# Preparing the delta-rule scan inside the projection loop, with low-rank products of 32 rows

## The chip, the cores and the metric

The kernel runs on one core of a Trainium2 chip. The metric is the device time of one execution in microseconds (us); a run's figure is the median of its executions. TensorE (PE) does the matrix products, VectorE (DVE), ScalarE (ACT) and GpSimd (POOL) the elementwise work, and SyncE (SP) issues the transfers from DRAM. Each engine executes its own queue in order; semaphores hold an instruction back until what it needs is there.

## The reference, cut to what matters

The whole program is two transformer-like blocks for 256 context and 256 latent tokens (512 columns together) of width 1024, in float32. The change touches only the mixer of the first block, which sends one projection through two state scans:

```
z = h @ w_in                                    # 1024 -> 26 tiles of 128 columns
z_rw = centred_shift(z[:, :RW_COLS], mu)         # delta rule ("rwkv") part
r, k, v, lw, la, lg = split(z_rw)
logw  = w0 + tanh(lw_d) @ w_up_d                 # two directions d, 32 -> 512
decay = exp(-exp(-softplus(-logw) - 0.5))
iclr  = sigmoid(a0 + la_d @ a_up_d)              # 32 -> 512
kk    = k * k_k / max(norm per head, 1e-12)
k_dir = k * (1 + (iclr - 1) * k_a)
delta-rule scan over (r, decay_d, k_dir_d, v, -kk, kk * iclr_d), forward and backward
zg, xbc, dt = split(z[:, RW_COLS:])              # state space ("mamba") part
xm, B, C = silu(conv(xbc));  chunked state space scan, forward and backward
out = concat([rwkv part, mamba part]) @ w_out
```

Behind the mixer come a gated feed-forward, a neighbourhood attention, a mixture of eight experts and two blocks of another kind; nothing in them is edited.

## The kernel before, in words

`mixer_in` runs over the 26 column tiles of the projection. For a tile b it splits the weights into a high and a low part (`split`, L347 on ACT and L348 on DVE), multiplies them with the split activations (`mm3`, L361, L362 and L364: 24 matmuls of 128x512), and shifts or convolves the result (L475 to L492). Tiles 0 and 1 hold the small inputs `lg`, 2 to 9 `xbc`, 10 to 13 `zg`, 14 to 17 k, 18 to 21 r, 22 to 25 v of the delta rule (`zrw`, 12 tiles).

Beside the tiles a generator, `mamba`, is advanced: L493 says by how many stages after which tile. It has 23 stages: 3 of set-up, taken at tiles 1, 3 and 5, then 20, of which one or two are taken after each tile from the 9th on:

```
for _ in range(1 if b in (1, 3, 5) else 0 if b < 9 else 1 if b % 3 else 2):
    next(beside, None)
```

Of these, `pre` transposes a token block, `seg` makes a decay matrix (L568 and L570 scale masks into `ta` on ACT and POOL, L571 multiplies them on PE, L573 takes the exponential), `out` multiplies (L580, L582), `carry` moves the state, `gate` (L615 to L618) and `group` (L624 to L630, with a reciprocal on DVE at L628) finish it.

`rwkv_prep` comes after the loop. It needs k and `lg` only, not r and v. It loads the low-rank weights `lora` (L650) and overwrites `lg[:, 0]` by a second load once `tl` has been made of it (L661), sums the squares of k per head with four products (L666, `sel`), takes root and reciprocal (L668 to L670), and for each of four column tiles j and two directions d makes: a low-rank product and sigmoid for the decay (L675, L677), its running sum in chunks of 64 (L679, a scan on DVE into `cs`), a low-rank product and sigmoid `ic` (L682, L683), `kd` = `ic` scaled and shifted (L685) times k (L686), and, once a product of 8 rows has spread the norms (L688) and k is normalised (L689), `b` = k times `ic` (L691, on POOL). The weights of each low-rank product are stored with zeros in the other 96 rows, so that every product reads all 128 rows of `tl`. The ring `pq` of two buffers holds the squares, the norms and the decay's sigmoids in turn; `ic0` and `ic1` have two buffers each.

`rwkv` then scans eight chunks. Its head fills `X` and `bkp` on POOL (L707, L709), and `products` makes `ew`, `ei`, `ar` and `bkp` (L732 to L741) for PE's first products (L750). Beside the scan the rows of the modulation (`ada`, L396 to L405) are computed from transfers of 256 KB each (L329).

Outside of `start`, Tile's scheduler sets each engine's order from a model of its own: it moves instructions across the program's order as their inputs come ready, so the order of the code is only its priority.

Of the kernel before, what the change touches and what calls it, by code (L numbers as in the profile page):

```python
# [11 lines left out]
F32 = mybir.dt.float32  # L12
F32R = mybir.dt.float32r
AF = mybir.ActivationFunctionType
ALU = mybir.AluOpType
# [3 lines left out]
P = 128  # L19
T = 512  # L20
# [73 lines left out]
def host_arrays(inp):  # L94
# [75 lines left out]
    lo = _Pack()  # L170
    for d in range(2):
        lo.add(f"w_up{d}", _rows_to(g["rw_w_up"][0, d], at=32 * d))
        lo.add(f"a_up{d}", _rows_to(g["rw_a_up"][0, d], at=64 + 32 * d))
    lo.add("g_up", _rows_to(g["rw_g_up"][0]))
# [91 lines left out]
class Net:  # L266
# [190 lines left out]
    def mixer_in(self, a, accs, zrw, xbc, zg, lg, pool, beside):  # L457
# [5 lines left out]
        for b in range(26):  # L463
# [20 lines left out]
            else:  # L484
# [6 lines left out]
                for d in range(2):  # L491
                    nc.vector.scalar_tensor_tensor(y, pad[:, :, 2 * d:2 * d + S], self.p(f"mu{d}", j), y,  # L492
                                                   op0=ALU.mult, op1=ALU.add)  # L493
            for _ in range(1 if b in (1, 3, 5) else 0 if b < 9 else 1 if b % 3 else 2):
                next(beside, None)
# [148 lines left out]


    def rwkv_prep(self, zrw, lg, arr, pool):
        nc = self.nc
        mm = nc.tensor.matmul
        lora = pool.tile([P, 2048], F32, name="lora", bufs=1)
        nc.sync.dma_start(lora, self.ins["lora"][:, :2048])  # L650
        o = {n: a for n, (a, _) in self.lora_at.items()}
        reset = pool.tile([P, T], F32, name="reset", bufs=1)
# [7 lines left out]
        nc.vector.tensor_scalar(ka1, self.p("k_a"), -1.0, 1.0, op0=ALU.mult, op1=ALU.add)  # L660
        nc.sync.dma_start(lg[:, 0], self.ins["lora"][:, 2048:2560])  # L661
        ssp = self.bank(2, [8, T])
        for j in range(4):
            kq = pool.tile([P, T], F32, name="pq")
            nc.scalar.activation(kq, zrw[:, j], AF.Square, scale=self.p("k_k", j))
            mm(ssp, self.c("sel")[:, 8 * j:8 * j + 8], kq, start=j == 0, stop=j == 3)  # L666
        nrm = pool.tile([8, T], F32, name="pq")
        nc.scalar.activation(nrm, ssp, AF.Sqrt)  # L668
        nc.vector.tensor_scalar(nrm, nrm, 1e-12, None, op0=ALU.max)
        nc.vector.reciprocal(nrm, nrm)  # L670
        for j in range(4):
            ic = [pool.tile([P, T], F32, name=f"ic{d}") for d in range(2)]
            for d in range(2):
                wp = self.bank(0, [P, T])
                mm(wp, lora[:, o[f"w_up{d}"] + j * P:o[f"w_up{d}"] + (j + 1) * P], tl, start=True, stop=True)  # L675
                sg = pool.tile([P, T], F32, name="pq")
                nc.scalar.activation(sg, wp, AF.Sigmoid, bias=self.p(f"w0{d}", j))  # L677
                back = slice(None, None, -1) if d else slice(None)
                nc.vector.tensor_tensor_scan(arr["cs"][:, d, j, back], reset, sg[:, back], 0.0,  # L679
                                             op0=ALU.mult, op1=ALU.add)  # L680
                ap = self.bank(1, [P, T])
                mm(ap, lora[:, o[f"a_up{d}"] + j * P:o[f"a_up{d}"] + (j + 1) * P], tl, start=True, stop=True)  # L682
                nc.scalar.activation(ic[d], ap, AF.Sigmoid, bias=self.p(f"a0{d}", j))  # L683
                kd = arr["kd"][:, d, j]
                nc.vector.tensor_scalar(kd, ic[d], self.p("k_a", j), ka1[:, j:j + 1], op0=ALU.mult, op1=ALU.add)  # L685
                nc.vector.tensor_mul(kd, kd, zrw[:, j])  # L686
            rp = self.bank(3, [P, T])
            mm(rp, self.c("selt")[0:8, j * P:(j + 1) * P], nrm, start=True, stop=True)  # L688
            nc.vector.scalar_tensor_tensor(zrw[:, j], zrw[:, j], self.p("k_k", j), rp, op0=ALU.mult, op1=ALU.mult)  # L689
            for d in range(2):  # L690
                nc.gpsimd.tensor_mul(arr["b"][:, d, j], zrw[:, j], ic[d])  # L691

    def rwkv(self, zrw, arr, lg, y, pool, fill):
# [256 lines left out]
    def layer0(self, run, late):  # L950
# [3 lines left out]
        with ExitStack() as mix:  # L954
            lgp = pool(mix, "lgp")
            scan = self.consts(mix, "scan")
            lg = lgp.tile([P, 2, T], F32, name="lg")
            zrw = pool(mix, "zp").tile([P, 12, T], F32, name="zrw")
            with ExitStack() as ph:
                self.stream(ph, 4, 1024, side="right")  # L960
                ap = pool(ph, "ap", side="right")
                with ExitStack() as first:
                    a, accs = self.start(zrw, xin, ap, first)
                self.places = cycle([self.raw])
                nc.sync.dma_start(scan, self.ins["cst_scan"])
                mw, mz = pool(ph, "mw", 2), pool(ph, "mz")
                xbc = mz.tile([P, 8, T], F32, name="xbc")
                zg = mz.tile([P, 4, T], F32, name="zg")
                self.mixer_in(a, accs, zrw, xbc, zg, lg, pool(ph, "zw", 2, "right"), self.mamba(xbc, zg, lg, cat, mw, mz))
            with ExitStack() as ph:  # L970
                self.stream(ph, RAWS, 512, 0, "right")
                arrp = pool(ph, "arr", side="right")
                arr = {k: arrp.tile([P, 2, 4, T], F32, name=k) for k in ("cs", "b", "kd")}
                with ExitStack() as c:
                    self.rwkv_prep(zrw, lg, arr, pool(c, "pw", 2))
                with ExitStack() as c:
# [1070 lines left out]
```

## Time and profile before

| what | value |
|---|---|
| median of 3 runs | 3050.53 us (3050.32 to 3051.49) |
| the profiled execution's own time | 3049.11 us |
| its span in the profile | 3047.3 us |
| busy: PE, DVE, ACT, POOL | 96%, 69%, 52%, 25% of the span |
| mean granted TensorE clock | 0.979 |

The profiled execution has its own time beside the span: 1.8 us lie around the span, and it is 1.4 us under the median. The shares are averages over stages with different limits, so they say little of one stage; a stage is read from its own window. A matmul's end is modelled, so that a PE that issues without a gap shows as fully busy.

### The profile page before, as it was taken

To read this page: it belongs to the slowest core of one execution; us is meant where nothing else is said; L and a number is where in the kernel's file an instruction comes from. 1 tells how busy PE (TensorE), PEld (TensorE's weight loads), DVE (VectorE), ACT (ScalarE), POOL (GpSimd) and SP (SyncE) were. 2 spreads that over 40 slices of the span, in tenths; PEclk is the share of its full clock that TensorE was granted. 3 is DMA by queue.
4 is the path that set the end of the run, shared out by engine and by line. 5 is a ranking of instruction groups with operands and counts; after the bars stand their busy time and mean duration, and the time that the engine had idled before them with its cause. 6 is when DMAs were issued, how large, how long until landed. Compare 5 with 4: busy or idle time off the path is not lost. (4 is left out here: it accounts for less than half of the span.)

```text
span 3047.3 us, 44960 instructions
## 1 busy us (share of the span) xinstructions
PE 2935.5 (96%) x17880; PEld 2453.4 (81%) x17880; DVE 2113.2 (69%) x2953; ACT 1592.5 (52%) x2007; POOL 774.2 (25%) x719
## 2 busy tenths in 40 slices
PE   7997899999999998999999999999999999999998
PEld 5884677887888777888888888878888888888887
DVE  5658987622223654998888898977697666669665
ACT  5644223432222555777777776755445545545553
POOL 0335442211022112000000000035264534434552
PEclk9998799999999999999999999999999999999999
DMA  6222234244423334999999999955533555553453
GB/s 229 70 66 70 84 111 148 104 166 146 137 75 114 110 97 154 346 359 331 363 345 337 357 350 362 340 176 186 197 132 120 192 175 199 170 195 107 150 176 128
DMA packets 132456, 584.75 MB, mean 192 GB/s; under 512 B 11792, under 2 KB 48912, under 8 KB 79760
## 3 DMA queue, kind: packets, MB, share of 16 engines
q1 hardware_dynamic: 126592, 575.35, 53.2%
q10 hardware_dynamic: 5648, 6.47, 0.9%
q8 instruction: 142, 2.33, 0.3%
q14 instruction: 74, 0.61, 0.1%
HBM read 580.73 MB, written 1.05 MB: 191 GB/s over the span
## 5 line engine op out<-in xcount | busy, mean ns | idle before, releaser
L348 DVE TENSOR_TENSOR wlo<-raw,whi 128x2048 fp32r<-128x2048 f32 (+2 forms) x497 | 1059.3, 2139 | 243.3 <-ACT whi L347 204.9
L347 ACT ACTIVATE whi<-raw 128x2048 fp32r<-128x2048 f32 (+2 forms) x500 | 886.5, 1784 | 418.8 <-PE bank L362 195.6
L372 PE MATMUL bank<-a,whi 128*128 128x512 f32 x1408 | 355.4, 395 | 5.1 <-DVE a L1693 5.1
L372 PEld LDWEIGHTS bank<-a,whi 128*128 128x128 f32 x1408 | 256.0, 190 | 51.7 <-DVE a L1693 5.4
L1361 PE MATMUL bank<-whi,xghi 128*128 128x512 f32 x704 | 282.3, 401 | 0.0
L1362 PE MATMUL bank<-whi,xglo 128*128 128x512 f32 x704 | 276.6, 393 | 0.0
L348 POOL TENSOR_TENSOR wlo<-raw,whi 128x2048 fp32r<-128x2048 f32 x3 | 13.9, 4646 | 790.2 <-ACT whi L347 790.2
L361 PE MATMUL bank<-cathi,whi 128*128 128x512 f32 (+1 forms) x608 | 212.6, 368 | 1.4 <-ACT x L1264 1.0
L362 PE MATMUL bank<-catlo,whi 128*128 128x512 f32 (+1 forms) x608 | 211.6, 364 | 1.5 <-DVE catlo L454 1.5
L375 PEld LDWEIGHTS bank<-a,wlo 128*128 128x128 f32 x1408 | 191.8, 190 | 13.6 <-DVE wlo L348 0.4
L375 PE MATMUL bank<-a,wlo 128*128 128x256 f32 x1408 | 196.5, 283 | 0.0
L1364 PE MATMUL bank<-wlo,xghi 128*128 128x512 f32 x704 | 192.2, 394 | 0.0
L1748 POOL TENSOR_TENSOR g<-gs,g 128x256 fp32r<-128x256 f32 x88 | 153.0, 1740 | 97.3 <-ACT g L1747 97.3
L372 PE MATMUL bank<-g,whi 128*128 128x512 f32 x704 | 171.2, 391 | 0.1
L1362 PEld LDWEIGHTS bank<-whi,xglo 128*128 128x128 f32 x704 | 132.4, 188 | 26.7
L1361 PEld LDWEIGHTS bank<-whi,xghi 128*128 128x128 f32 x704 | 132.2, 188 | 27.0
L1364 PEld LDWEIGHTS bank<-wlo,xghi 128*128 128x128 f32 x704 | 129.9, 188 | 29.6 <-DVE wlo L348 2.1
L372 PEld LDWEIGHTS bank<-g,whi 128*128 128x128 f32 x704 | 128.4, 188 | 24.4 <-POOL g L1748 0.3
L1613 PE MATMUL bank<-whi,gthi 128*128 128x512 f32 x352 | 139.7, 397 | 0.0
L361 PEld LDWEIGHTS bank<-cathi,whi 128*128 128x128 f32 x608 | 114.7, 190 | 29.3 <-issue 8.3
L1613 PE MATMUL bank<-whi,gtlo 128*128 128x512 f32 x352 | 138.1, 392 | 0.0
L364 PE MATMUL bank<-cathi,wlo 128*128 128x512 f32 (+1 forms) x608 | 136.4, 362 | 0.0
(530 smaller groups left out, 5883.1 us busy)
## 6 DMA issues: line engine op xcount, KB each, us to landing
raw<-in_moei_dram SPq DMA_DIRECT2D x155, 1024.0 KB, 5.7
raw<-in_sfi_dram SPq DMA_DIRECT2D x88, 1024.0 KB, 4.8
raw<-in_moeo_dram SPq DMA_DIRECT2D x77, 1024.0 KB, 5.2
raw<-in_sfo_dram SPq DMA_DIRECT2D x64, 704.0 KB, 4.1
raw<-in_ada_dram SPq DMA_DIRECT2D x104, 256.0 KB, 3.6
raw<-in_smi_dram SPq DMA_DIRECT2D x24, 1024.0 KB, 4.8
raw<-in_ffi_dram SPq DMA_DIRECT2D x22, 1024.0 KB, 4.9
x<-in_moei_dram SPq DMA_DIRECT2D x21, 1024.0 KB, 5.8
```

Of the source, the lines that this page charges most:

```text
L347: self.nc.scalar.activation(like(hi, w)[:, c], w[:, c], AF.Copy)
L348: (eng or self.nc.vector).tensor_sub(like(lo, w)[:, c], w[:, c], like(hi, w)[:, c].bitcast(F32))
L361: mm(ps, l, a[0][:, ak[j]], start=start and j == 0, stop=False, skip_group_check=True)
L362: mm(ps, l, a[1][:, ak[j]], start=False, stop=False, skip_group_check=True)
L364: mm(ps, w[1][:, wk[j], f0:f0 + fn], a[0][:, ak[j]], start=False, stop=stop and j == n - 1, skip_group_check=True)
L372: mm(ps.rearrange("p i s -> p (i s)"), w[0][:, wk[j], f0:f0 + P], a[:, ak[j]].rearrange("p i s -> p (i s)"), start=start and j == 0, stop= ...
L375: mm(ps[:, 0], w[1][:, wk[j], f0:f0 + P], a[:, ak[j], 0], start=False, stop=stop and j == n - 1, skip_group_check=True)
L1361: mm(ps, a[0][:, at + k, rows], w[0][:, k, cols], start=start and n == 0, stop=False, skip_group_check=True)
L1362: mm(ps, a[1][:, at + k, rows], w[0][:, k, cols], start=False, stop=False, skip_group_check=True)
L1364: mm(ps, a[0][:, at + k, rows], w[1][:, k, cols], start=False, stop=stop and n == len(ks) - 1, skip_group_check=True)
L1613: mm(y[f], g.bitcast(F32) if self.whole else g, w[q][:, i, 512 * f:512 * f + 512], start=n == q == i == p == 0, stop=n == 10 and i == 1 an ...
L1748: nc.gpsimd.tensor_sub(lo, s, hi.bitcast(F32))
```

## The change

Five things change. The preparation `rwkv_prep` becomes a generator of five pieces (one for the norms, one for each j) and is appended to `mamba` in a generator `beside`; the step table gives two stages to each of tiles 9 to 18 and one to each after, so the pieces belong to tiles 19 to 23. The low-rank weights are packed without the zeros, 32 rows of each of the four products, and each product reads its own 32 rows of weights and of `tl`, into four PSUM banks (1, 1, 2, 2 instead of 0 and 1). `kd`'s scale and shift moves from DVE to ACT. The norms get a buffer of their own. The arrays `cs`, `b` and `kd` lie where the state space scan's tiles were.

```
@@ host_arrays
     lo = _Pack()
-    for d in range(2):
-        lo.add(f"w_up{d}", _rows_to(g["rw_w_up"][0, d], at=32 * d))
-        lo.add(f"a_up{d}", _rows_to(g["rw_a_up"][0, d], at=64 + 32 * d))
+    lo.add("up", np.concatenate([g["rw_w_up"][0, 0], g["rw_w_up"][0, 1], g["rw_a_up"][0, 0], g["rw_a_up"][0, 1]]))
@@ mixer_in
-            for _ in range(1 if b in (1, 3, 5) else 0 if b < 9 else 1 if b % 3 else 2):
+            for _ in range(1 if b in (1, 3, 5) else 0 if b < 9 else 2 if b < 19 else 1):
                 next(beside, None)
@@ rwkv_prep
-        lora = pool.tile([P, 2048], F32, name="lora", bufs=1)
-        nc.sync.dma_start(lora, self.ins["lora"][:, :2048])
-        o = {n: a for n, (a, _) in self.lora_at.items()}
+        lora = pool.tile([P, 512], F32, name="lora", bufs=1)
+        nc.sync.dma_start(lora, self.ins["lora"][:, :512])
...
-        nrm = pool.tile([8, T], F32, name="pq")
+        nrm = pool.tile([8, T], F32, name="nrm", bufs=1)
...
+        yield
         for j in range(4):
             ic = [pool.tile([P, T], F32, name=f"ic{d}") for d in range(2)]
+            low = [self.bank(k, [P, T]) for k in (1, 1, 2, 2)]
+            for n, r in enumerate(low):
+                q = slice(32 * n, 32 * n + 32)
+                mm(r, lora[q, j * P:(j + 1) * P], tl[q], start=True, stop=True)
             for d in range(2):
-                wp = self.bank(0, [P, T])
-                mm(wp, lora[:, o[f"w_up{d}"] + j * P:o[f"w_up{d}"] + (j + 1) * P], tl, start=True, stop=True)
                 sg = pool.tile([P, T], F32, name="pq")
-                nc.scalar.activation(sg, wp, AF.Sigmoid, bias=self.p(f"w0{d}", j))
+                nc.scalar.activation(sg, low[d], AF.Sigmoid, bias=self.p(f"w0{d}", j))
...
-                ap = self.bank(1, [P, T])
-                mm(ap, lora[:, o[f"a_up{d}"] + j * P:o[f"a_up{d}"] + (j + 1) * P], tl, start=True, stop=True)
-                nc.scalar.activation(ic[d], ap, AF.Sigmoid, bias=self.p(f"a0{d}", j))
+                nc.scalar.activation(ic[d], low[2 + d], AF.Sigmoid, bias=self.p(f"a0{d}", j))
                 kd = arr["kd"][:, d, j]
-                nc.vector.tensor_scalar(kd, ic[d], self.p("k_a", j), ka1[:, j:j + 1], op0=ALU.mult, op1=ALU.add)
+                nc.scalar.activation(kd, ic[d], AF.Identity, scale=self.p("k_a", j), bias=ka1[:, j:j + 1])
                 nc.vector.tensor_mul(kd, kd, zrw[:, j])
...
                 nc.gpsimd.tensor_mul(arr["b"][:, d, j], zrw[:, j], ic[d])
+            yield
@@ layer0
-                mw, mz = pool(ph, "mw", 2), pool(ph, "mz")
+                states, prep = ExitStack(), ExitStack()
+                mw, mz = pool(states, "mw", 2), pool(states, "mz")
...
-                self.mixer_in(a, accs, zrw, xbc, zg, lg, pool(ph, "zw", 2, "right"), self.mamba(xbc, zg, lg, cat, mw, mz))
-            with ExitStack() as ph:
-                self.stream(ph, RAWS, 512, 0, "right")
-                arrp = pool(ph, "arr", side="right")
-                arr = {k: arrp.tile([P, 2, 4, T], F32, name=k) for k in ("cs", "b", "kd")}
-                with ExitStack() as c:
-                    self.rwkv_prep(zrw, lg, arr, pool(c, "pw", 2))
+                arr = {}
+
+                def beside():
+                    yield from self.mamba(xbc, zg, lg, cat, mw, mz)
+
+                    states.close()
+                    arrp = pool(scans, "arr")
+                    arr.update({k: arrp.tile([P, 2, 4, T], F32, name=k) for k in ("cs", "b", "kd")})
+                    yield from self.rwkv_prep(zrw, lg, arr, pool(prep, "pw", 2))
+
+                self.mixer_in(a, accs, zrw, xbc, zg, lg, pool(ph, "zw", 2, "right"), beside())
+                prep.close()
+            with scans:
+                self.stream(scans, RAWS, 512, 0, "right")
                 with ExitStack() as c:
                     rw = pool(c, "rw", 2)
```

Where this puts instructions is seen in each engine's order. On PE before, at the end of the projection (L362 and L364 are its last tile, L666 the sums of squares, L675 and L682 low-rank products, L688 the norms, L396 the modulation; at the "..." lie more of the kinds of L666 to L688):

```order
L362 MATMUL bank_1946<-alo,whi 128x512
L364 MATMUL bank_1946<-ahi,wlo 128x512 x8
L666 MATMUL bank_2008<-pq,cst_scan 8x512 x2
L675 MATMUL bank_2027<-tl,lora 128x512
L682 MATMUL bank_2032<-tl,lora 128x512
...
L688 MATMUL bank_2128<-pq,cst_scan 128x512
L682 MATMUL bank_2113<-tl,lora 128x512
...
L675 MATMUL bank_2118<-tl,lora 128x512
L396 MATMUL bank_2956<-raw,c_59 32x256 x8
```

On PE in the changed kernel, from the third tile from the end to the modulation (its L359, L360 and L362 are the projection, L664 the sums, L675 all low-rank products, L687 the norms, L394 the modulation; at the "..." lie the rest of that tile and the last two with 3 sums, 9 low-rank products and 2 products of the norms among them):

```order
L362 MATMUL bank_1991<-ahi,wlo 128x512 x3
L664 MATMUL bank_1773<-pq,cst_scan 8x512
L675 MATMUL bank_1830<-tl,lora 128x512
...
L675 MATMUL bank_1961<-tl,lora 128x512
L362 MATMUL bank_2094<-ahi,wlo 128x512 x7
L687 MATMUL bank_1980<-nrm,cst_scan 128x512
L675 MATMUL bank_2025<-tl,lora 128x512
L675 MATMUL bank_2027<-tl,lora 128x512
L675 MATMUL bank_1963<-tl,lora 128x512
L675 MATMUL bank_2026<-tl,lora 128x512
L394 MATMUL bank_2956<-raw,c_59 32x256 x8
L687 MATMUL bank_2045<-nrm,cst_scan 128x512
```

All 24 products of the preparation stood behind the projection before. From the first sum on, 53 matmuls of the projection come after it in this queue; 4 sums, 11 low-rank products and 2 products of the norms stand among them, and 2 products of the norms and 5 low-rank ones behind them. One low-rank product (bank_2028) still follows the last row shown.

On DVE in the changed kernel, the end of the preparation (L680 is the scan, L685 `kd` times k, L688 the normalised k, L490 the shift of the projection's last tile, L738 the delta-rule scan's first products):

```order
L688 SCALAR_TENSOR_TENSOR zrw<-zrw,par,bank_1915 128x512
L490 SCALAR_TENSOR_TENSOR zrw<-pad,par,zrw 128x512 x2
L680 SCALAR_TENSOR_TENSOR cs<-reset,pq 128x512
L685 TENSOR_TENSOR kd<-kd,zrw 128x512 x2
L680 SCALAR_TENSOR_TENSOR cs<-reset,pq 128x512
L688 SCALAR_TENSOR_TENSOR zrw<-zrw,par,bank_1980 128x512
L685 TENSOR_TENSOR kd<-kd,zrw 128x512
L688 SCALAR_TENSOR_TENSOR zrw<-zrw,par,bank_2045 128x512
L403 TENSOR_TENSOR mod_67<-bank_2957,par 128x4
L738 TENSOR_TENSOR bkp<-b,ei 64x4x64
```

The last two normalised k stand one instruction apart, so that POOL has the last four `b` to do behind them; in the kernel before, three scans (L679), two products (L686) and one L685 lay between.

## Rows read from the trace of the kernel before

**Rows 1.** Windows by stage: us A:B, length; busy us of PE, PEld, DVE, ACT, POOL; clock; DMA.

```profile
105.00:221.00 116.00, 116.00 (x655) 100.52 (x654) 61.89 (x83) 60.65 (x98) 47.09 (x66) 1.00 0.18 60
221.00:233.20 12.20, 12.20 (x52) 9.09 (x51) 8.41 (x9) 3.28 (x6) 0.14 (x2) 1.00 0.20 64
233.20:268.40 35.20, 25.20 (x65) 7.77 (x64) 32.72 (x35) 19.74 (x29) 13.32 (x6) 0.90 0.06 20
268.40:280.50 12.10, 8.90 (x55) 6.85 (x55) 2.62 (x6) 2.22 (x7) 11.74 (x17) 0.60 0.33 116
```

**Rows 2.** Timeline of PE: start us, us, line, operation, count [idle before, its releaser].

```profile
233.17 1.88 PE L666 MATMUL bank<-pq,cst_scan 128*8 128x512 f32 x4
...
244.14 1.88 PE L682 MATMUL bank<-tl,lora 128*128 128x512 f32 x4
245.95 1.98 PE L688 MATMUL bank<-pq,cst_scan 8*128 8x512 f32 x4
...
258.60 1.12 PE L675 MATMUL bank<-tl,lora 128*128 128x512 f32 x2 [1.78 <-ACT pq L677]
263.61 1.93 PE L396 MATMUL bank<-raw,c 128*32 128x256 f32 x16 [3.88 <-ACT pq L677]
...
280.49 2.05 PE L750 MATMUL bank<-ar,bkp 128*128 128x128 f32 x16
```

**Rows 3.** Groups on DVE, 233.2 to 268.4 us: count, busy us, mean ns, idle before.

```profile
L679 DVE TENSOR_TENSOR_SCAN cs<-reset,pq 128x512 f32<-128x512 f32 x8 | 10.8, 1363 | 0.0
L686 DVE TENSOR_TENSOR kd<-kd,zrw 128x512 f32<-128x512 f32 x8 | 7.4, 929 | 0.1
L685 DVE TENSOR_SCALAR kd<-ic,par,ka 128x512 f32<-128x512 f32 x8 | 6.1, 766 | 1.2 <-ACT ic L683 1.2
```

**Rows 4.** Timeline of DVE: weight split and mamba's last group, then the preparation's end.

```profile
221.15 1.16 DVE L348 TENSOR_TENSOR wlo<-raw,whi 128x1024 fp32r<-128x1024 f32 x1
222.23 1.40 DVE L630 SCALAR_TENSOR_TENSOR x<-yfm,par,ysc 128x512 f32<-128x512 f32 x2
...
230.33 3.35 DVE L628 RECIPROCAL ysc<-ysc 128x512 f32<-128x512 f32 x1 [0.51 <-ACT ysc L627]
233.72 1.42 DVE L630 SCALAR_TENSOR_TENSOR x<-yfm,par,ysc 128x512 f32<-128x512 f32 x2
...
267.62 0.72 DVE L689 SCALAR_TENSOR_TENSOR zrw<-zrw,par,bank 128x512 f32<-128x512 f32 x1
...
273.71 0.52 DVE L738 TENSOR_TENSOR bkp<-b,ei 64x256 f32<-64x256 f32 x1 [3.41 <-POOL bkp L709]
```

**Rows 5.** Timeline of POOL, 233 to 275 us.

```profile
260.72 5.29 POOL L691 TENSOR_TENSOR b<-zrw,ic 128x512 f32<-128x512 f32 x2 [4.37 <-DVE zrw L689]
268.49 2.52 POOL L691 TENSOR_TENSOR b<-zrw,ic 128x512 f32<-128x512 f32 x2 [2.47 <-ACT ew L732]
270.92 1.01 POOL L707 MEMSET X<- 128x512 f32 x2
271.85 1.83 POOL L709 MEMSET bkp<- 128x2048 f32 x1
```

**Rows 6.** One line's instructions: L691 on POOL, ns min/median/max, first and last start.

```profile
L691 POOL TENSOR_TENSOR b<-zrw,ic x8: 1297/1976/3127, 248.3 to 269.7; 128x512 f32<-128x512 f32 x8
```

**Rows 7.** Groups on ACT and POOL for L570 and L573, 105 to 233 us.

```profile
L570 POOL TENSOR_SCALAR ta<-cst_all,av 128x128 f32<-128x128 f32 x26 | 19.7, 764 | 28.7 <-PE bank L571 28.7
...
L573 ACT ACT_TABLE_LOAD x4 | 5.1, 1283 | 0.1
L573 ACT ACTIVATE eseg<-bank 128x512 f32<-128x512 f32 x8 | 4.8, 598 | 1.3 <-PE bank L571 1.2
```

**Rows 8.** Timeline of SP's queue: the loads of lora and lg, and the modulation's.

```profile
195.15 0.37 SPq L650 DMA_DIRECT2D lora<-in_lora_dram  x1
202.16 0.33 SPq L661 DMA_DIRECT2D lg<-in_lora_dram  x1
```

**Rows 9.** Timeline of PE in the scan: products on the two halves of the rows.

```profile
359.84 0.22 PE L804 MATMUL bank<-st,hh 64*64 64x64 f32 x1
359.85 0.22 PE L832 MATMUL bank<-uv,g 64*64 64x64 f32 x1
```

**Rows 10.** Groups on ACT, 233.2 to 268.4 us: the decay's sigmoids.

```profile
L677 ACT ACTIVATE pq<-bank,par 128x512 f32<-128x512 f32 x8 | 5.4, 686 | 8.9 <-DVE cs L679 8.9
```

**Rows 11.** The experts' count read on SP's queue (L1494), ns, start.

```profile
L1494 SPq TENSOR_LOAD <-most x1: 476/476/476, 1239.5 to 1239.5; - x1
```

More of the change, by code (lines that the diff above doesn't have):

```diff
@@ L660, in rwkv_prep @@
         nc.vector.tensor_scalar(ka1, self.p("k_a"), -1.0, 1.0, op0=ALU.mult, op1=ALU.add)
-        nc.sync.dma_start(lg[:, 0], self.ins["lora"][:, 2048:2560])
+        nc.sync.dma_start(lg[:, 0], self.ins["lora"][:, 512:1024])
         ssp = self.bank(2, [8, T])
@@ L958, in layer0 @@
             zrw = pool(mix, "zp").tile([P, 12, T], F32, name="zrw")
+            scans = ExitStack()
             with ExitStack() as ph:
```

## The prediction

> **What bounds the kernel now.** I read the windows first. From 105 to 221 us, the projection with the state space scan beside it, PE issues without a gap (116.00 of 116.00 us) while DVE is at 61.89, ACT at 60.65 and POOL at 47.09: that stage is as long as its matmuls [rows 1]. From 233.2 to 268.4 us, the preparation, it is the other way round: DVE 32.72 of 35.20 us, PE 25.20 [rows 1]. PE's timeline shows the turn: the projection's last matmul is followed at 233.17 us by the sums of squares, and later low-rank products wait for ACT's sigmoids, which wait for a buffer that DVE's scans free [rows 2, 10]. DVE's timeline ends the stage: the last normalised k starts at 267.62 us, POOL makes the last two `b`, fills `X` and `bkp`, and DVE's next instruction waits for that fill until 273.71 us; PE's first products of the scan start at 280.49 us [rows 2, 4, 5]. The path is therefore projection on PE, preparation on DVE, a tail on POOL. What moves the fill of `bkp` (ended at 273.68) moves everything behind it, since the later stages begin when this one hands over.
>
> **The change part by part.**
>
> *Earlier start.* 53 matmuls of the projection stand behind the first product of the preparation now. From 221.0 to 233.2 us the trace has 52 matmul records, all but two of them the projection's and those two nearly twice as long [rows 1], so the preparation's first product can issue at about 221.0, 12.2 us earlier, if the same matmuls take the same time up to there. They do if two scan stages a tile hide like one or two: the table gives 20 stages to 10 tiles instead of 15, and PE's sum is unchanged.
>
> *PE.* A product of 512 columns in this format is two instructions; four take 1.81 us from 244.14 to 245.95 [rows 2], so 0.86 us a product plus a little. 17 of them (4 sums, 11 low-rank, 2 norms) now stand among the projection: 14.6 us. Without overlap the projection ends at 221.0 + 12.2 + 14.6 = 247.8. Behind it come 2 norms and 4 low-rank ones ahead of the last normalised k, 5.2 us, and eight modulation products, 1.93 us at the most [rows 2]: 254.9. The low-rank ones have 32 rows instead of 128, but as many columns, and I take the same 0.86 us. No row has four groups of 32 rows; the nearest are products on the two halves of the rows, which start 0.01 us apart and so overlap [rows 9]. The lower bound is four for the price of one: 9.3 us of PE less at the most (the eleven clusters in the order allow about 4), the upper bound 0.86 each plus a cost per change of shape. From a product of 128 rows to one of 8 rows, 245.95 is 0.09 us later than four steps of 0.43 from 244.14 would give [rows 2]; 22 such changes are 2 us. I take 1 us of both together, as the stretch is held by DVE.
>
> *DVE.* From 221.0 to 268.4 it was busy 8.41 + 32.72 = 41.1 us of 47.4 and idle 6.3 [rows 1]. Off go the eight L685, 6.1 us [rows 3], and mamba's last norms, 1.40 + 3.35 + 1.42 = 6.2 us [rows 4], which is now done before. One more weight split falls into the stretch, 1.2 us [rows 4]. That leaves 30.0 us. With the same idle time the last normalised k ends at 221.0 + 30.0 + 6.3 = 257.3, against 268.3: 11.0 us earlier. With no idle time it would be 251.0, but PE cannot deliver its input before 254.9; so 255.6 to 257.3, and I take 257.3, since scan and `kd` keep the durations that they had beside POOL (means 1363 and 929 ns [rows 3]).
>
> *POOL's tail.* Before, one pair of `b` lay behind the last normalised k: 268.34 to 271.01 us [rows 5]. Now two pairs do, because the last two normalised k stand one product apart. A `b` takes 1.30 us alone and up to 3.13 beside DVE [rows 6]; the pair that ran with DVE idle took 2.52, the one before 5.29 [rows 5]. From the third normalised k, 1.7 us earlier (255.6), one pair at 3.4 and one at 2.52 end at about 261.5 instead of 271.0. The gain shrinks from 11.0 to 9.5 us; the bounds are 255.6 + 5.0 and 255.6 + 10.6, a gain of 10.4 or 4.8. The fills behind (1.01 and 1.83 us) stay.
>
> *ACT.* Eight `kd` at the price of a sigmoid, 0.69 us [rows 10], are 5.5 us more. ACT was busy 19.74 of 35.20 us and waited 8.9 us for DVE's scans because the norms held one of the two `pq` buffers [rows 1, 10]; with their own buffer that wait is the cover. Cover gone, it would be 5.5 us at most. Three more table loads by the order of ACT (24 against 21), 1.28 us each [rows 7], fall where ACT is half idle: nothing.
>
> *Transfers.* `lora` shrinks to a quarter and was issued at 195.15 us behind the last weights of the projection, 39 us before use [rows 8]. The reload of `lg` waits for `tl`, which ACT makes later now, and the modulation's loads stand behind it on SP; first use of those is behind the preparation, over 25 us on. Nothing. In the expert stage one weight load stands behind a read of 0.48 us instead of ahead of it [rows 11], and some order differs there: I allow 3 us either way, as I find no wait behind it.
>
> *Sum.* 12.2 earlier; the preparation from its first product to POOL's last `b` 261.5 - 221.0 = 40.5 us instead of 271.0 - 233.2 = 37.8; minus 0.5 for the shapes: 9.0 us. The profiled execution took 3049.11 us, its span and 1.8 around it; 3040.1 by that. It is 1.4 us under the median, so the median comes to **3041.5 us**.
>
> A rule speaks against mixing shapes: the Trainium skill's "TensorEngine Tiling (Array Packing)", Tiling Modes, says that a change of tiling mode drains TensorE. The 0.09 us at 245.95 [rows 2] is all that this trace shows of it; by a full drain at every change the 2 us above would grow, and by the trace they don't.
>
> **The rivals.**
>
> *More is gained* (0.17). The four row groups overlap and DVE's waits vanish: PE's part falls by about 4 us, the last normalised k comes at 252 to 253, and POOL's pairs run nearly alone (5.2 us): `b` ends at 257, a gain of 14: 3036.5 us. For it speaks that two row halves start in one instant [rows 9]; against it, that only the last j has its four products side by side in the order. The same page's statement that tiles work in parallel agrees with rows 9 as far as they go.
>
> *POOL takes over* (0.23). With `b` beside a busy DVE all the time, eight at up to 3.13 us [rows 6] are 25 us. The first normalised k needs 8 low-rank products, 4 sums and one norm (11.2 us), some 36 projection matmuls (8.3 us) and itself (0.7): 241.2 at the earliest. `b` then ends at 266 to 268, a gain of 3 to 5 us: 3046.5 us, within 0.2%, which is about what a measurement of this kernel can tell from no change. For it: POOL's times vary by two and a half. Against: half of them lie where DVE waits.
>
> *PE stalls in the denser scan* (0.06, slower). The chain of one `seg` and `out` is four `ta` on POOL at 0.76 us, an exponential of 0.60 with a table load of 1.28 on ACT [rows 7], two products on DVE and PE's own: some 7 us. A tile with two stages has 24 matmuls, 5.5 us, and two stages of PE work, about as much again by my estimate (116 us hold some eleven tiles and three quarters of the scan [rows 1]); POOL waited for PE before, 28.7 us [rows 7], not the reverse. If the order leaves PE idle for 2.4 us in each of the ten tiles, 24 us are lost against 9 won: 3065 us. It decides against the change from 1.5 us a tile on.
>
> **How the numbers follow.** The forecast, 3041.5 us, has 0.54. Its own range is 3038 to 3046, from POOL's bounds and the 3 us of reordering. The range of 8 in 10 reaches over most of both neighbours, 3033 to 3049.5. Faster by over 0.2% (under 3044.4): most of the forecast, the larger gain and a little of POOL's case, 0.70. Within 0.2%: 0.24. Slower: 0.06.
>
> **What would show it.** Right: the first sum of squares near 221 us, the projection's last matmul near 248, no idle PE before; the last normalised k near 257, `b` ending near 261 and the first product of the scan near 271; later stages shifted by the same 9 us. Wrong: PE waiting for `ta`, exponentials or sums between 115 and 221 us; low-rank products overlapping four at a time; `b` on POOL as the last releaser after 265 us; or a stage behind the mixer that takes back what the mixer gave.

## The result and the profile after

The changed kernel takes 3069.12 us (median of 4 runs, 3067.93 to 3071.31) where the kernel before took 3050.43 on the same chips: a ratio of 1.0061, 95% interval 1.0049 to 1.0073. It is **slower by 18.7 us**; 3041.5 was predicted. The profiled execution took 3067.97 us, its span 3066.1. A profile shows one execution, and those of one kernel lie up to 13 us apart, so a profile that lies far from its kernel's median is named as such below.

Set out by stages, with the start of the same instruction as the boundary in both profiles (us; the last two boundaries are 1200 and 2010 us of before, 1214.7 and 2029.0 after; the sum is 19.0, the spans differ by 18.8):

| stage | before | after | difference |
|---|---|---|---|
| start to the first product of the delta-rule scan (L750) | 280.5 | 279.1 | -1.4 |
| to the first `st` times `z` of the scan's first chunk (L836) | 62.4 | 66.8 | +4.4 |
| to that of the fifth chunk | 116.2 | 115.0 | -1.2 |
| to that of the eighth | 81.3 | 88.9 | +7.6 |
| to the first mix-out product (`cathi`) | 7.2 | 13.9 | +6.7 |
| on to the experts | 652.4 | 651.0 | -1.4 |
| the experts | 810.0 | 814.3 | +4.3 |

The windows of the changed kernel up to the scan (columns as in [rows 1]; the first answers to the first of [rows 1], the others to its rest):

```profile
105.00:221.00 116.00, 116.00 (x657) 100.17 (x656) 70.62 (x90) 65.48 (x103) 50.04 (x66) 1.00 0.17 53
222.20:246.10 23.90, 23.90 (x73) 10.64 (x73) 14.90 (x15) 15.66 (x21) 0.81 (x3) 1.00 0.11 33
246.10:256.60 10.50, 10.50 (x20) 4.00 (x18) 4.47 (x5) 4.05 (x6) 2.23 (x3) 0.51 0.00 0
256.60:279.10 22.50, 13.78 (x85) 8.43 (x84) 10.23 (x15) 10.97 (x20) 16.52 (x21) 0.70 0.30 94
```

PE has no gap until 256.6. But in the third row its granted clock is 0.51, almost all of the stretch at the lower of the two levels, 1.2 GHz, and it does 20 matmuls in 10.5 us where the row above does 73 in 23.9. PE's timeline says which (columns as in [rows 2], to which it answers; L664 are the sums of squares, L675 the low-rank products, 32 rows each):

```profile
222.22 1.02 PE L664 MATMUL bank<-pq,cst_scan 128*8 128x512 f32 x2
223.17 1.12 PE L675 MATMUL bank<-tl,lora 32*128 32x512 f32 x2
...
225.18 1.13 PE L675 MATMUL bank<-tl,lora 32*128 32x512 f32 x4
...
251.40 2.07 PE L675 MATMUL bank<-tl,lora 32*128 32x512 f32 x2
```

A product is two instructions: at full clock one takes 1.05 us alone, at half clock 2.0. DVE and POOL end the stage as before, late (answers to [rows 4, 5]):

```profile
263.58 0.72 DVE L688 SCALAR_TENSOR_TENSOR zrw<-zrw,par,bank 128x512 f32<-128x512 f32 x1
...
265.00 0.75 DVE L688 SCALAR_TENSOR_TENSOR zrw<-zrw,par,bank 128x512 f32<-128x512 f32 x1
...
272.40 0.52 DVE L738 TENSOR_TENSOR bkp<-b,ei 64x256 f32<-64x256 f32 x1 [1.34 <-POOL bkp L709]
```

```profile
264.38 5.32 POOL L690 TENSOR_TENSOR b<-zrw,ic 128x512 f32<-128x512 f32 x4 [5.71 <-DVE zrw L688]
...
270.56 1.81 POOL L709 MEMSET bkp<- 128x2048 f32 x1
```

Then the scan. Its windows, with the boundaries of the table, before:

```profile
280.50:342.90 62.40, 48.57 (x499) 35.99 (x500) 59.34 (x227) 14.44 (x33) 33.09 (x46) 0.75 0.41 139
...
459.10:540.40 81.30, 77.51 (x1039) 61.67 (x1038) 61.44 (x196) 31.06 (x61) 20.10 (x24) 1.00 0.39 137
540.40:547.60 7.20, 5.58 (x76) 4.36 (x76) 3.37 (x10) 4.68 (x8) 1.81 (x4) 1.00 0.00 0
```

and after:

```profile
279.10:345.90 66.80, 47.20 (x498) 35.65 (x496) 62.81 (x219) 14.98 (x34) 35.59 (x48) 0.79 0.39 127
...
460.90:549.80 88.90, 82.86 (x1041) 65.32 (x1040) 59.02 (x197) 27.57 (x52) 20.76 (x24) 0.90 0.24 78
549.80:563.70 13.90, 6.48 (x77) 4.97 (x77) 9.32 (x21) 8.93 (x17) 1.82 (x4) 0.87 0.56 220
```

In the first chunk DVE is the bound in both kernels, and 62.81 us of its work instead of 59.34 lie ahead of the first L836: its queue holds the scan in another order. That the order costs the 4.4 us of this stretch is not shown: with the first kernel's order it took 65.9, 66.2 and 65.0 us in runs 4, 9 and 10 below. In the last three chunks PE is the bound, with as many matmuls as before at a lower clock. The last row is a third thing: DVE and ACT have two to three times the work, while PE waits. Two things come late there, a load on SP's queue (waits: who for whom, us in total, times, longest; and the timeline) and the splits on ACT:

```profile
SPq L327 <- PE bank L854: 39.5, 1, 39.5
```

```profile
554.94 11.39 SPq L327 DMA_DIRECT2D raw<-in_mixout_dram  x4
```

```profile
558.06 2.17 ACT L947 ACTIVATE cathi<-x 128x512 fp32r<-128x512 f32 x4
...
561.74 1.91 ACT L345 ACTIVATE whi<-raw 128x2048 fp32r<-128x2048 f32 x1
```

Before, both came beside the scan:

```profile
504.36 46.36 SPq L329 DMA_DIRECT2D raw<-in_mixout_dram  x4
```

```profile
523.42 1.15 ACT L947 ACTIVATE cathi<-x 128x512 fp32r<-128x512 f32 x2 [3.97 <-PE bank L903]
```

Now the load waits for the scan's last products (L854), which read tiles in the same memory, and `cathi` stands in ACT's queue behind the scan's last outputs; run 6 shows that the second holds the mix-out without the first. The experts lose their 4.3 us in one place, where PE waits 2.17 us for a sum on DVE (L1562) that before was no wait, with the clock at half for 3.4 us behind it:

```profile
1637.77 0.50 PE L1561 MATMUL bank<-back,yg 128*128 128x256 f32 x2 [2.17 <-DVE x L1562]
```

### The profile page after: what moved, and what is told of

Its sections match the earlier page's. It is cut to its first block, busy times and chain, and to the rows that moved or that the text cites. A ratio compares the mean times of both kernels' runs of the same rounds, so it can differ in the third digit from the quotient of the medians.

```text
span 3066.1 us, 44964 instructions
## 1 busy us (share of the span) xinstructions
PE 2949.4 (96%) x17880; PEld 2462.4 (80%) x17880; DVE 2112.6 (69%) x2945; ACT 1604.2 (52%) x2018; POOL 773.5 (25%) x719
## 3 DMA queue, kind: packets, MB, share of 16 engines
HBM read 579.94 MB, written 1.05 MB: 189 GB/s over the span
## 5 line engine op out<-in xcount | busy, mean ns | idle before, releaser
L359 PE MATMUL bank<-cathi,whi 128*128 128x512 f32 (+1 forms) x608 | 214.1, 368 | 1.0 <-ACT x L1273 1.0
L360 PE MATMUL bank<-catlo,whi 128*128 128x512 f32 (+1 forms) x608 | 212.6, 363 | 1.4 <-DVE catlo L452 1.4
L359 PEld LDWEIGHTS bank<-cathi,whi 128*128 128x128 f32 x608 | 114.8, 190 | 28.8 <-issue 8.3
L362 PE MATMUL bank<-cathi,wlo 128*128 128x512 f32 (+1 forms) x608 | 136.9, 362 | 0.0
```

What stands on the lines that cost most here:

```text
L359: mm(ps, l, a[0][:, ak[j]], start=start and j == 0, stop=False, skip_group_check=True)
L360: mm(ps, l, a[1][:, ak[j]], start=False, stop=False, skip_group_check=True)
L362: mm(ps, w[1][:, wk[j], f0:f0 + fn], a[0][:, ak[j]], start=False, stop=stop and j == n - 1, skip_group_check=True)
```

## The experiments

Three theories stood after the two traces. **P**: the arrays' place, left instead of right, puts what the mix-out needs where the scan's last tiles lie. **C**: narrow products among the projection lower the clock. **S**: the scheduler's other order of the scan's queues loses the time. Orders and addresses are those of the built programs. "Scan order of before" means that PE's first 1200 instructions from the scan's start stand in the very order of the kernel before; in the changed kernel another product stands at 350 of these 1200 places.

**1. Place alone** (on the kernel before; scan order of before).

```diff
-                arrp = pool(ph, "arr", side="right")
+                arrp = pool(ph, "arr")
```

> The kernel before with one thing of the change alone: the arrays cs, b and kd lie on the left side of the memory, under the scan's tiles, where the change puts them; nothing is moved in time. Theory P (placement): the scan's last tiles (g, uv, st, z) now lie where the mix-out weights and cathi are to land, so the first mix-out load waits for the scan's last products (L854) as in the changed kernel, where it was issued at 554.9 against 504.4, and the first mix-out product comes some 6 us late: 3056 to 3058 us; up to 3066 if the whole loss of 16 us between the first scan product and the first mix-out product is of this kind. Theory C (the clock falls among narrow products beside the projection) and theory S (the scan's order changes because the preparation was moved): nothing is moved here, so 3050, within 3 us.

Measured: 3065.45 us, ratio 1.0047 (1.0030 to 1.0064). The wait and the late load are there with nothing moved in time:

```profile
SPq L329 <- PE bank L854: 41.0, 1, 41.0
```

```profile
466.90:546.60 79.70, 76.38 (x1036) 61.07 (x1035) 57.05 (x189) 27.31 (x52) 20.19 (x24) 1.00 0.27 87
546.60:562.00 15.40, 8.29 (x77) 6.53 (x77) 9.32 (x21) 8.94 (x17) 1.82 (x4) 0.69 0.51 198
```

15.4 us from the last L836 to the first mix-out product instead of 7.2, the scan itself unharmed. The other half is not the mix-out: the first scan product started 5.6 us later (286.1), since the preparation's first sums did (238.75 against 233.17; they waited for ACT, which made `tl` there ahead of the squares), and the experts lost 4.3. P holds for the 8 us; the forecast that theories C and S had here, 3050, is a miss.

**2. The preparation's edits alone** (on the kernel before: row groups, `kd` on ACT, `nrm`; nothing moved).

```diff
-                wp = self.bank(0, [P, T])
-                mm(wp, lora[:, o[f"w_up{d}"] + j * P:...], tl, start=True, stop=True)
+                mm(r, lora[q, j * P:(j + 1) * P], tl[q], start=True, stop=True)
...
-                nc.vector.tensor_scalar(kd, ic[d], ...)
+                nc.scalar.activation(kd, ic[d], AF.Identity, ...)
```

> The kernel before with the preparation's own edits (row groups of 32, kd on ACT, nrm in a tile of its own) and nothing moved in time or place. Theory P: DVE loses 6 us of kd and the wait for pq of 8.9 us goes, so the preparation gains 4 to 8 us and the end with it: 3042 to 3047. Theory C: the narrow products now follow one another without the projection's between them, the clock falls by 246 instead of 261 and takes part of it back: 3047 to 3055. Theory S: no forecast nearer than 3040 to 3060.

Measured: 3050.59 us, ratio 1.0002 (0.9992 to 1.0011). C's forecast: the clock fell at 243.2 instead of 261.1 and stayed at half for 34 us (the windows' clock column: 0.66 and 0.50 from 240 to 260), and the first scan product started at 279.7, only 0.8 earlier. PE had waited 0.78 us just ahead of this fall. The profile is the slowest of ten executions (3056.64 us), with a second fall at 482.1 for 24 us; the time of 3042 to 3047, which P had forecast, is a miss.

**3. The table alone** (on the kernel before, two stages to tile 18).

```diff
-            for _ in range(1 if b in (1, 3, 5) else 0 if b < 9 else 1 if b % 3 else 2):
+            for _ in range(1 if b in (1, 3, 5) else 0 if b < 9 else 2 if b < 19 else 1):
```

> The kernel before with the new table of steps alone: two stages of the state space scan a tile, the preparation still behind the projection. Theories P and C: TensorE had no idle time up to 221 in either kernel, so 3050, within 2 us. Rival: the denser scan costs by itself, then slower by 3 us or more, with the projection's end later than 233.2.

Measured: 3059.87 us, ratio 1.0036 (1.0026 to 1.0047): a miss for P and C, and at first sight the rival's time. Yet the first scan product started at 281.0, as before; the time went in the scan (66.7, 114.2 and 90.9 us by the table's rows instead of 62.4, 116.2 and 81.3). PE's order there is the changed kernel's, all 1200, though no line of the scan differs.

**4. The same table to tile 16** (`b < 17` in place of `b < 19`): the scan order of before.

> The kernel before with the table of steps alone, but two stages a tile only as far as tile 16 instead of 18. The scan of the state space is as dense in the tiles where it is dense; what differs from the run with 18 is that VectorE's, ScalarE's and GpSimd's queues hold the delta-rule scan in the very order of the kernel before, where that run held it in the changed kernel's. Theory S (order): 3048 to 3052, and the first L836 about 62.5 us after the first L750 as before, not 66.6. Rival (the denser state space scan costs by itself): 3056 to 3061 as with 18.

Measured: 3051.74 us, ratio 0.9996 (0.9987 to 1.0006). The time is S's; of its detail the first chunk is a miss, 65.9 us and not 62.5, with the clock at 0.72 in that stretch. The difference from run 3 lies in the last three chunks, here first with the table to 16, then to 18:

```profile
462.20:543.80 81.60, 77.48 (x1036) 61.59 (x1035) 61.20 (x199) 30.97 (x61) 20.48 (x25) 1.00 0.40 137
```

```profile
461.90:552.80 90.90, 85.58 (x1040) 67.47 (x1039) 61.91 (x202) 31.25 (x61) 20.39 (x24) 0.89 0.36 123
```

**5. The change with the table to 16** (the changed kernel, scan order of before).

> The changed kernel with the same table to tile 16: the preparation still beside the projection's last tiles, the arrays still on the left, and the delta-rule scan's queues in the order of the kernel before but for some five places. Theory S: the 4 to 5 us that the first chunk of the scan lost and what followed from them go: 3057 to 3063 against 3069. Theory P (placement) alone: 3067 to 3071.

Measured: 3055.20 us, ratio 1.0010 (1.0000 to 1.0020); by the ratios 0.5 of 0.6% are back, more than S had forecast. In the profile the first scan product started at 276.2, 4.3 us ahead of before, and the scan kept that lead: the last L836 at 533.1 against 540.4. Then the mix-out took 12.3 us instead of 7.2, and the experts lost 4.2 again. But this profile took 3048.69 us, 6.5 under the median: four of the ten executions took 3046.9 to 3050.9 at a mean granted clock of 0.978 or 0.979, six 3055.2 to 3059.8 at 0.973 or 0.974. So the lead that the profile kept is that of the four; where the clock fell in the six was not profiled.

**6. The same with the tiles placed otherwise.**

```diff
+        for name, shape, n in (("X0", [P, 4, P], 1), ("X1", [P, 4, P], 1), ("ar", [P, 2, 4, P], 3), ...):
+            for _ in range(n):
+                pool.tile(shape, F32, name=name, bufs=n)
...
-            self.stream(ph, 3, pairs=3, side="right")
+            wp = pool(ph, "wsplit", 3, "right")
+            self.stream(ph, 3, pairs=0, side="right")
```

> The run before this one with the scan's tiles placed otherwise: those used last lie lowest, those done early (bkp, ew, ei, c, s, lb, lm, adar) where cathi and catlo come to lie, and the mix-out's raw buffers under its split ones. Theory P: cathi need not wait for the scan's last products, is written before 550, and the first mix-out product follows the last L836 within 9 us (7.2 before, 13.9 in the changed kernel): 5 to 8 us less than the run before this one, 3050 to 3057. Rival: ScalarE's queue or the load holds it as before, no difference within 2 us.

Measured: 3050.88 us, ratio 0.9996 (0.9986 to 1.0005), but not for the reason expected: the stretch to the mix-out took 12.2 us, as in run 5. The load was issued early, and ACT's queue still holds the splits behind the scan's last outputs:

```profile
530.38 18.88 SPq L327 DMA_DIRECT2D raw<-in_mixout_dram  x4
```

```profile
539.70 0.46 ACT L938 ACTIVATE go<-bank,par 128x128 f32<-128x128 f32 x1 [1.89 <-PE bank L934]
540.06 2.18 ACT L953 ACTIVATE cathi<-x 128x512 fp32r<-128x512 f32 x4
```

The two profiles, 3046.6 and 3046.0 us of span, don't tell where the small difference of the medians is from; the clocks of the executions go with it: at 0.973 or 0.974 ran six of run 5's ten, one of these ten. In the built program `cathi` lies here in the memory of `bkp`, `ei`, `ew`, `lmask` and `tt`, none of which the scan reads last; in the changed kernel it lies in that of `st`, `uv` and `vr`, among others. With the arrays on the left, the late load is thus not the whole of it; the splits' place in ACT's queue holds the mix-out by itself, and what gives them that place was not found. **7.** The changed kernel with a like re-placing (and the table to 18) told the same:

> The changed kernel with another placement alone: the scan's tiles that are done early (bkp, ew, ei, c, s, lb, lm, adar, lmask) lie lowest, and the mix-out's raw buffers under its split ones, so that the first mix-out load needs only tiles that are done long before the scan's end. Theory P: the first mix-out load is issued before 530, the idle 5.4 us of TensorE ahead of the first mix-out product go: 3061 to 3064 against 3069. Theories C and S: the loss lies elsewhere and stays, 3067 to 3071.

Measured: 3071.02 us, ratio 1.0071 (1.0054 to 1.0087); the load at 518.6 us, the stretch 13.9 us as in the changed kernel. P's remedy is a miss in both, though in run 7 `cathi` still lies in the memory of `st`, `uv` and `vr`. A layout with the preparation beside the projection and the arrays on the right was not tried: the projection's buffers are there.

**8. Whole rows** (the changed kernel, weights padded with zeros to 128 rows as before).

```diff
-                mm(r, lora[q, j * P:(j + 1) * P], tl[q], start=True, stop=True)
+                mm(r, lora[:, q:q + P], tl, start=True, stop=True)
```

> The changed kernel with the low-rank products over all 128 rows (the weights padded with zeros, as in the kernel before) instead of row groups of 32; placement, table and the scan's order are the changed kernel's. Theory C: TensorE's clock does not fall at 246 for 10 us, the projection ends by 251 and not 256, the first scan product comes 4 to 6 us earlier: 3062 to 3066. If the clock falls there with whole rows too, the row groups are not the cause: 3067 to 3072.

Measured: 3065.21 us, ratio 1.0038 (1.0026 to 1.0051). The clock stays where it fell:

```profile
246.10:256.60 10.50, 10.50 (x43) 4.88 (x41) 9.29 (x8) 8.37 (x14) 5.06 (x4) 1.00 0.01 3
```

43 matmuls in place of 20 in the same 10.5 us, the first scan product at 274.8 instead of 279.1. C is shown: only 12 of PE's 986 products ahead of the scan stand elsewhere than in the changed kernel, and in each of the six profiles with 32-row products the clock fell at 243 to 249 us, while in the three with the same products over whole rows (runs 8 to 10) it held to 255 to 262. Its price is 4.3 us in this pair of profiles, but it varies: in run 12, with row groups and the changed kernel's order up to there, the clock was at half for 6.8 us instead of 10.2 and the first scan product came at 275.2.

**9. Whole rows, `nrm` and `kd` in place** (run 2 with whole rows and the table to 16).

> The kernel before, the preparation behind the projection and the arrays on the right as there, with the table to tile 16, nrm in a tile of its own, kd on ACT and the four low-rank products of a tile together, but over all 128 rows; the scan's and the experts' queues stand in the order of the kernel before. Theories P, C and S together: no narrow products, so the clock does not fall before 255 (in the run with row groups and nothing moved it fell at 243 for 34 us); the preparation loses the wait for pq and 4 us of DVE, the first scan product comes 3 to 6 us earlier and nothing behind it gives that back: 3043 to 3048, faster than both kernels. If the clock falls at 243 here too, narrow rows are not its cause, and the time is 3049 to 3052.

Measured: 3050.18 us, ratio 0.9994 (0.9986 to 1.0003). The clock held to 255.2 and the scan began 2.7 us earlier, but the median is the same as before within the interval, and the forecast of 3043 to 3048 is a miss. The profile can't say why: it is the slowest of twelve executions (3057.94 us), in which the clock fell at 483.9 and the last three chunks took 90.9 us with the order of before; nine of the twelve took 3046.1 to 3052.1. **10.** Whole rows in the changed kernel, with the table to 15 (`b < 16`, and not to 16 as the expectation says; with whole rows the built scan has the order of before with that table):

> The changed kernel with whole rows as in the run on them, and the table to tile 16, which with whole rows puts the scan's queues into the order of the kernel before. Theory S and C: the first scan product some 5 us earlier than in the kernel before, the scan as long as there, 4 to 5 us lost again at the mix-out (placement) and up to 4 in the experts (their queue order is the changed kernel's): 3047 to 3053 against 3065 with the same whole rows in the other order. If only the placement counts, 3060 or more.

Measured: 3062.97 us, ratio 1.0035 (1.0022 to 1.0048), a miss in size: with that table, which leaves the state space scan more tiles, the preparation started at 230.1, and the scan at 281.8. The scan took as long as before (260.7 from L750 to the last L836), the stretch to the mix-out 15.4, the experts lost 4.3. So the scan bore S out, and the rest was given back by a late start and the place.

**11 and 12. The wait filled.** What makes the clock fall in the last three chunks? Ahead of each fall stands one wait, here in the changed kernel and, shorter and with no fall behind it, in run 4:

```profile
487.94 0.52 PE L758 MATMUL bank<-cst_all,bkp 64*128 64x64 f32 x9 [1.65 <-DVE g L751]
```

```profile
487.55 0.58 PE L758 MATMUL bank<-cst_all,bkp 64*128 64x64 f32 x10 [0.46 <-DVE g L751]
```

All four profiles with the changed kernel's order had the wait of 1.65 us, and a fall within 3 us of it that lasted 17 to 24 us; the eight with the order of before had 0.45 to 0.48 us, and two fell (runs 2 and 9, both the slowest execution of their kernel). The wait's length alone does not decide it: the changed kernel waited 1.63 us at 465.47 too, ahead of modulation products, and the clock stayed. Two products that nobody reads were put at that place in the kernel of run 3 and in the changed kernel. PE's order is the same up to them; behind them, against what the expectations say, the scheduler moved more: of the 380 products to the scan's last L836 over 100 stand in another order, some by 30 places or more:

```diff
+            if n == 7:
+                fp = self.bank(1, [P, T])
+                for _ in range(2):
+                    mm(fp, ident, zrw[:, 8], start=True, stop=True, skip_group_check=True)
```

> The kernel before with the new table (two stages to tile 18), and two products on TensorE whose result nobody reads, placed in the last chunk's products just where TensorE waited 1.65 us for VectorE (at 486.8 to 488.4 in the run with the table alone); all queues otherwise in that run's order. In all four profiles with that order the clock fell to half right behind this wait, for 17 to 24 us; in the eight with the order of the kernel before, whose wait there is 0.46 us, in two. Theory: the wait makes the clock fall, and that is what the order costs: with the wait filled the clock stays, the stretch from the fifth to the eighth L836 takes 82 us instead of 90.9, and the time is 3050 to 3054 instead of 3060. Rival: the order costs by its work, or the clock falls for another reason: 3058 to 3062, 1 us more for the two products.

> The changed kernel with the same two products at the same place. Theory: the clock stays behind the wait, and 7 to 9 us of the 18.8 come back: 3060 to 3063. Rival: 3068 to 3072.

Measured: 3056.42 us, ratio 1.0015 (1.0005 to 1.0024), and 3056.71 us, ratio 1.0026 (1.0016 to 1.0036), against 1.0036 and 1.0061 without. Behind the filled wait the clock held in both; in the changed kernel:

```profile
482.46 1.98 PE L756 MATMUL bank<-zrw,cst_all 128*128 128x512 f32 x4
484.38 0.58 PE L762 MATMUL bank<-cst_all,bkp 64*128 64x64 f32 x6
```

```profile
457.40:536.60 79.20, 76.38 (x1044) 61.16 (x1043) 58.34 (x196) 27.08 (x52) 20.90 (x24) 1.00 0.27 88
```

79.2 us instead of 88.9, with more matmuls; 82.9 instead of 90.9 in the other:

```profile
465.20:548.10 82.90, 78.09 (x1047) 62.43 (x1046) 62.20 (x204) 30.98 (x61) 20.92 (x24) 0.98 0.39 135
```

There the clock did fall later, at 535.1 for 3.4 us, behind a new wait of 2.35 us. So the wait and the clock's fall go together at this place, and removing the one removed the other twice; that the wait is the cause, and not the order of the products behind it, which moved with it, is argued and not shown. Run 11 is above the expected 3054 because its experts lost 4.2 us, which run 3's did not. Run 12 is below its expected 3060: of the 12.1 us between its profile and the changed kernel's, 3.9 came ahead of the scan, where PE's order is the same, and 9.7 in the last three chunks, with some lost again at the mix-out (16.9 us). Across all profiles the experts lose 3.0 to 4.7 us at the one wait for a sum on DVE exactly where ACT's queue there differs from the first kernel's (ten of ten; 25 or more of some 500 instructions stand in another order), and nothing where it doesn't (three of three). What gives the scheduler one order or the other was not found; on the first kernel, with the table to tile 15, 17 or 18 the built scan has the changed kernel's order, with it to 16 the first kernel's.

## Why the prediction was wrong, point by point

The forecast was a gain of 9.0 us, measured is a loss of 18.7. Some 7.6 of the 27.6 us between them lie ahead of the scan's first product (1.4 us earlier instead of 9.0), the other 20 behind it.

- *Earlier start*: right. PE had no gap from 105 to 221, the first sum of squares came at 222.22 (221.0 predicted). The rival "PE stalls in the denser scan" named the right sign for a reason that did not occur, which is luck.
- *PE*: **failed** in its duration. Its 0.86 us a product was read at full clock; the projection ended at 256.6, not 247.8. Of the 8.8 us, 5.1 are 10.2 us at half clock and 1.2 the later start; the other 2.5 are not separated (lone 32-row products at 1.05 us are part of it). Pairs side by side did overlap, two in 1.06 us, as the rival "More is gained" wanted, but there were only two such pairs before the clock fell. The step allowed 1 us for shapes "as the stretch is held by DVE"; from 222.2 to 256.6 PE held it, busy without a gap while DVE was busy 19.4 of 34.4 us.
- *DVE*, *POOL's tail*: carried the lateness on. The last normalised k ended at 265.75 (257.3 predicted), `b` at 269.70 (261.5). From the third normalised k, POOL took 5.4 us, 5.9 predicted; it had waited 5.71 us for that k, so the rival "POOL takes over" did not occur. *ACT* cost nothing that shows.
- *Transfers*, "Nothing": **failed**. The step asked what was issued in another order around the preparation, not what lands later in the memory that the arrays gave up or the scan moved into. Measured: 6.7 us at the mix-out here, 5 to 10 in the seven other profiles with the arrays on the left, none with them on the right (run 2, whose profile lost 1.3, aside).
- *Sum*, by "What moves the fill of `bkp` moves everything behind it": **the step that failed most**. It took the stages behind as rigid. In run 5's profile the scan did carry a lead of 4.3 us to its end; in the changed kernel, with the scheduler's other order, the scan to its last L836 took 10.8 us longer, 7.6 of it in the last three chunks, where the clock was at half for 17.1 us from the end of one wait of 1.65 us on (with the wait filled, runs 11 and 12 got 8.0 and 9.7 back), and the experts 4.3, for which "3 us either way" was too little. With the order of before (runs 5 and 6) the time was the first kernel's within 0.1%, though the mix-out still lost 5 us there.
- *Shapes.* A product of 32 rows between whole ones took 1.05 us instead of 0.86, and about 0.1 us more was lost on either side of it (0.33 us between two starts instead of 0.23): some 0.4 us for a change in and one out, or 0.2 each, where the prediction read 0.09 from a change to 8 rows. The Trainium skill's "TensorEngine Tiling (Array Packing)", Tiling Modes, which was weighed, states a drain of TensorE at a change of mode. The trace agrees with a small one: 0.2 us a change, little beside the clock.

## What to carry to other kernels

Where a scheduler orders the queues and pools share memory, compare the whole built program, not the stage that was edited: the order of later stages, and which late readers lie under the next stage's first loads and writes. A change of under one per cent is judged only together with these, and a test that restores the old order or the old place with the edit kept in costs one line. Where a matrix engine is the bound, look in its clock column for what a wait of a microsecond or a run of narrow products does to the stretch behind it. And before a profile explains a median, compare its time and clock with those of the other executions: here three of the profiles lay 6 to 8 us from the median of their kernel.

## What the runs showed of the hardware that was not expected

- TensorE's clock fell from 2.4 to 1.2 GHz while PE issued without a gap, among products of 32 and 8 rows: at 246.1 us in the changed kernel, at 246.8 to 248.9 in runs 5, 6, 7 and 12. In run 2 it fell at 243.2, behind a wait of 0.78 us. With 128 rows in the same places it held to 262.3 (run 8), 255.2 (run 9) and 258.1 (run 10).
- In the scan's products of 64 rows, a wait of 1.65 us was followed by 17 to 24 us at half clock in four of four profiles, one of 0.45 to 0.48 us in two of eight. With the wait filled by products that nobody reads there was no fall at that place in two of two; a wait of 2.35 us later in run 11 was followed by 3.4 us at half clock, and one of 1.63 us at 465.47 in the changed kernel by none.
- Two 32-row products in different row groups, neighbours in the queue, took 1.06 us together (225.18 to 226.24); one alone took 1.05, more than a product over all 128 rows (0.86).
